# Token-major projections 512 columns at a time with four accumulators in the second layer, two first units side by side, and weights in half tiles

## The chip, the cores and the metric

The kernel runs on one core of one Trainium2 chip. The metric is the device time of one execution in microseconds (us); lower is better. A kernel's time is the median of several runs. The profile is of one further execution, and its times are the ones that a trace can explain line by line.

## What is computed

A trunk of two layers over 1024 tokens of width 1024, all in float32. Layer 0 projects the normed input and feeds a gated DeltaNet group and a sparse attention group (an indexer selects keys by score); layer 1 feeds a stick-breaking attention group and an HGRN2 gated recurrence. In each layer the two groups' outputs are concatenated and projected, and a SwiGLU FFN follows. Each mixer and each FFN is wrapped in two RMS norms, one ahead of it and one on its output before the residual is added:

```python
def rms_norm(x, g, eps=1e-6):
    xf = x.astype(jnp.float32)
    y = xf * lax.rsqrt(jnp.mean(xf * xf, axis=-1, keepdims=True) + eps)
    return (y * g.astype(jnp.float32)).astype(x.dtype)
...
    h = x
    for l in range(DEPTH):
        y = rms_norm(h, norm_g[l, 0])
        ...
        h = h + rms_norm(y, norm_g[l, 1])
        y = swiglu(rms_norm(h, norm_g[l, 2]), w_gate[l], w_up[l], w_down[l])
        h = h + rms_norm(y, norm_g[l, 3])
    return h
```

The even mixer's projection has 4176 columns, the odd one's 3584 (q, k, v of 512 each for the sticks; q, f, i and the output gate of 512 each for HGRN2). The FFN's inner width is 2816.

## The kernel before, in words

**Halves and tiles.** The 1024 tokens are worked on in two halves of 512. Activations lie feature-major: a half of h or y is 8 tiles of 128 features x 512 tokens. Weights come from HBM in "units" of 128 x 1024 floats, 422 in all; `wload` (L228) loads one raw unit (`wraw`) and splits it into a high part `whi` (ScalarE, L193) and a rest `wlo` (L197: VectorE for the first 512 columns, GpSimd for the second). Activations are split in the same way (`yhi`, `ylo`, or `act`). A product is then three passes on TensorE: high x high, low x high, high x low, added in one PSUM accumulator. `passes` (L240) issues them, at L251.

**Two kinds of projection.** `dense_fm` (L264) makes a feature-major result: one unit, one accumulator of 128 x 512, 24 matmuls of 512 columns. `dense_tm` (L270), called by `tm_store` (L541), makes a token-major one: 256 columns of the weights at a time, two accumulators each holding two token tiles, 48 matmuls of 256 columns to a unit. Four units make one token-major projection. In the second layer these are VC (values of the sticks, of both halves), ID (HGRN2's input) and GD (its gate); `tm_store` scales each result by the row form of the norm, passes it through a `stage` tile (two buffers) and stores it to HBM.

**PSUM.** There are 8 banks. `self.banks(acc=3, a=1, b=1, w=3)` in `run` (L1283) gives 3 to the accumulators, 1 to the recurrences' tag "a", 1 to tag "b", 3 to the attention's tag "w". Tiles of one tag are given out in the order in which the program asks for them: a tile waits until the one that had its bank before is read out.

**Norms.** A norm sums squares over the 8 feature tiles: ScalarE squares (L298), VectorE adds (L299, `ssq`). `inv_rms` (L302) adds over the partitions with one matmul by ones (L306), and ScalarE makes the inverse root by Ln and Exp (L308, L309); `inv_rms_rows` (L312) makes the same as a column for each token tile with four one-column matmuls (L317). Bank "b" serves them in `norms` (L346), `residual` (L376: scale L388, add h L389, store, then either make y's parts at once, L336, or square for the next norm) and `last_residual` (L504: L515, L516). The outputs of the output projection and the FFN are first gathered in `part` tiles by ScalarE (L429) or VectorE (L480, in the last FFN half L500).

**What sets the order.** The program is written half by half in `run`. A scheduler then lays out each engine's instructions by data, priorities (`with self.first()` gives a high one) and its own simulation; each engine runs its instructions in that order. So a matmul on bank "b" may be laid out far behind or ahead of matmuls on the accumulators, while two matmuls that start tiles of one tag keep the program's order. In the second layer the written order is: output projection of the first layer's second half, its residual, C projections (`proj_c`), sticks, FFN, its residual, second layer's output projection of half 0 (its first two quarters written ahead of that residual's second part), `proj_c(1)`, `proj_d(1)`, sticks and recurrence of half 1, FFN, output projection of half 1, and the last FFN, which goes by column halves (`down_halves`) with `last_residual` behind it.

## Time and profile before

| | |
|---|---|
| time, median of 3 runs (lowest to highest) | 2910.11 us (2907.5 to 2910.74) |
| the profiled execution's own time | 2903.69 us |
| its span on the core | 2901.9 us |
| mean granted TensorE clock | 0.992 |
| ScalarE busy | 1574.0 us (54%) |
| GpSimd busy | 1123.3 us (39%) |
| data moved by the hardware queue | 363.97 MB, 39.6% of its engines' span |

A row of the profile names the engine (PE is TensorE's matmuls, PEld its weight loads, DVE VectorE, ACT ScalarE, POOL GpSimd, SP the engine that issues the DMAs), the line, the tile written and the tiles read, the shape, and a count. A float32 matmul that is not split, such as a norm's by ones, stands as two records. In the timeline the first number is the start in us, the second the length; brackets give the idle time before a row and what ended it. In a view by windows each engine has its busy time and its count.

### The profile page before, as it was taken

What the parts mean: (1) busy time and instruction counts of PE and PEld (TensorE: products, weight loads), DVE (VectorE), ACT (ScalarE), POOL (GpSimd) and SP (SyncE); (2) the same over time, 40 slices, a digit from 0 to 9 for tenths busy, and PEclk for the clock granted to TensorE, in tenths of its full rate; (3) what the DMA queues carried; (4) which work ended last, traced back from release to release, by engine and by line L of the source; (5) the groups of instructions that cost most, each with busy time, mean ns of one, the idle gap of its engine ahead of it and who ended that gap; (6) DMA issues with size and microseconds to landing.
All of it is one profiled execution on the core that took longest, in us unless ns stands there. A gap on an engine that the chain in (4) does not pass through costs nothing. (4 is left out here: it accounts for less than half of the span.)

```text
span 2901.9 us, 41648 instructions
## 1 busy us (share of the span) xinstructions
PE 2818.6 (97%) x14850; PEld 2351.2 (81%) x14850; DVE 1694.5 (58%) x3037; ACT 1574.0 (54%) x2893; POOL 1123.3 (39%) x916
## 2 busy tenths in 40 slices
PE   8999999999999998999999999999999999999997
PEld 6888888878787886978788888889778778788886
DVE  7857973675656557378665235736666544732235
ACT  5545863666657585254664335536666544543333
POOL 3323332344435342255554332325555432333332
PEclk9999999999999999999999999999999999999999
DMA  5433446243333334446333334654323323543233
GB/s 196 136 121 109 144 151 209 91 146 114 103 117 107 104 121 137 139 147 202 111 109 95 100 97 125 231 156 128 98 87 107 98 89 115 167 149 98 95 95 109
DMA packets 200975, 366.63 MB, mean 126 GB/s; under 512 B 16544, under 2 KB 104640, under 8 KB 200768
## 3 DMA queue, kind: packets, MB, share of 16 engines
q1 hardware_dynamic: 200768, 363.97, 39.6%
q8 instruction: 117, 1.92, 0.3%
q14 instruction: 90, 0.74, 0.1%
HBM read 306.23 MB, written 57.67 MB: 125 GB/s over the span
## 5 line engine op out<-in xcount | busy, mean ns | idle before, releaser
L197 POOL TENSOR_TENSOR wlo<-wraw,whi 128x512 fp32r<-128x512 f32 x422 | 589.1, 1396 | 1240.3 <-PE acc L251 497.3
L193 ACT ACTIVATE whi<-wraw 128x512 fp32r<-128x512 f32 x844 | 521.6, 625 | 487.0 <-PE acc L251 431.2
L197 DVE TENSOR_TENSOR wlo<-wraw,whi 128x512 fp32r<-128x512 f32 x422 | 337.9, 801 | 470.7 <-PE acc L251 355.5
L251 PE MATMUL acc<-yhi,whi 128*128 128x512 f32 x2064 | 585.3, 400 | 11.8 <-ACT whi L193 8.0
L251 PE MATMUL acc<-ylo,whi 128*128 128x512 f32 x2064 | 581.9, 398 | 2.2 <-DVE ylo L336 2.2
L251 PE MATMUL acc<-yhi,wlo 128*128 128x512 f32 x2064 | 536.1, 396 | 0.0
L251 PE MATMUL acc<-act,whi 128*128 128x512 f32 (+1 forms) x1984 | 510.6, 393 | 21.3 <-DVE stage L452 5.7
L251 PEld LDWEIGHTS acc<-yhi,whi 128*128 128x128 f32 x2064 | 386.1, 189 | 99.5 <-ACT whi L193 8.0
L251 PEld LDWEIGHTS acc<-ylo,whi 128*128 128x128 f32 x2064 | 386.3, 189 | 88.3 <-issue 6.0
L251 PEld LDWEIGHTS acc<-yhi,wlo 128*128 128x128 f32 x2064 | 383.7, 188 | 84.1 <-issue 6.1
L251 PEld LDWEIGHTS acc<-act,whi 128*128 128x128 f32 x1984 | 363.1, 189 | 109.3 <-issue 11.5
L251 PE MATMUL acc<-act,wlo 128*128 128x512 f32 (+1 forms) x992 | 266.6, 386 | 1.4 <-POOL wlo L197 1.4
L251 PEld LDWEIGHTS acc<-act,wlo 128*128 128x128 f32 x992 | 182.0, 188 | 38.5 <-POOL wlo L197 1.8
L950 ACT ACTIVATE pen<-sc,tk 128x384 bf16<-128x384 f32 (+4 forms) x155 | 155.3, 1002 | 52.2 <-DVE tk L954 46.1
L480 DVE TENSOR_TENSOR part<-acc,part 128x512 f32<-128x512 f32 x152 | 103.8, 685 | 66.2 <-PE acc L251 66.0
L193 ACT ACTIVATE act<-stage 128x512 fp32r<-128x512 f32 x104 | 65.2, 629 | 136.9 <-DVE stage L459 117.0
L197 POOL TENSOR_TENSOR act<-stage,act 128x512 fp32r<-128x512 f32 x88 | 120.2, 1366 | 43.1 <-ACT act L193 41.0
L299 DVE TENSOR_TENSOR ssq<-ssq,sq 128x512 f32<-128x512 f32 (+1 forms) x119 | 98.7, 830 | 27.2 <-ACT sq L298 25.0
L951 DVE TENSOR_SCALAR tk<-tk 128x1 uint32<-128x1 f32 x186 | 39.3, 211 | 125.4 <-ACT pen L950 124.9
L452 DVE TENSOR_TENSOR stage<-acc,stage 128x512 f32<-128x512 f32 x66 | 45.5, 689 | 98.3 <-ACT stage L220 98.2
L251 PE MATMUL acc<-whi,yhi 128*128 128x256 f32 x640 | 100.1, 287 | 1.6 <-DVE stage L552 1.6
L251 PE MATMUL acc<-whi,ylo 128*128 128x256 f32 x640 | 101.3, 287 | 0.0
(461 smaller groups left out, 4038.1 us busy)
## 6 DMA issues: line engine op xcount, KB each, us to landing
wraw<-in_w_units_dram SPq DMA_DIRECT2D x422, 512.0 KB, 3.6
h<-part SPq DMA_DIRECT2D x40, 256.0 KB, 3.9
hld<-h SPq DMA_DIRECT2D x40, 256.0 KB, 4.6
qkvT<-stage SPq DMA_DIRECT2D x24, 256.0 KB, 2.5
kT<-kbT SPq DMA_DIRECT2D x24, 256.0 KB, 3.6
vv<-vb SPq DMA_DIRECT2D x24, 256.0 KB, 3.0
qkv<-qkvT SPq DMA_DIRECT2D x18, 256.0 KB, 3.6
part<-in_x_dram SPq DMA_DIRECT2D x16, 256.0 KB, 6.3
```

Of the source, the lines that this page charges most:

```text
L193: nc.scalar.activation(hi, src, AF.Copy)
L197: e.tensor_tensor(out=lo[:, c], in0=src[:, c], in1=hi[:, c].bitcast(F32), op=OP.subtract)
L251: mm(ps, l, r, start=first and g not in begun, stop=last and end[g] == i)
L299: nc.vector.tensor_tensor(out=acc, in0=acc, in1=sq, op=OP.add)
L452: nc.vector.tensor_tensor(out=s, in0=pg, in1=s, op=OP.mult)
L480: nc.vector.tensor_tensor(out=parts[d], in0=ps, in1=parts[d], op=OP.add)
L950: sc.activation(pen, s, AF.Sign, scale=sg, bias=nb, accum_out=n)
L951: v.tensor_scalar(rej.bitcast(U32), n, th, float(1 << b), op0=OP.is_lt, op1=OP.mult)
```

## The change

Layer 1 (from the point where the first layer's pools close) gets four accumulators and no bank "b". The norms that are made there use the accumulators' tag (`self.nb`); the first layer keeps bank "b". With four accumulators `tm_store` calls `dense_tm4`: all 512 columns at once, one accumulator for each token tile, 24 matmuls of 512 columns to a unit. The weights of that projection are read in other pieces from the same units. The raw weights come as two half tiles of 128 x 512 with a DMA each. `passes` takes its high pass in `steps` parts with the sums side by side, and its low pass one sum after the other. At the start of the kernel `dense_pair` runs two units (KI and the first QKV unit) side by side, in eight steps; the constants `cc` are loaded behind the first half's x.

```diff
@@ -156,7 +156,6 @@
         self.gg = self.t(cp, [P, G_COLS], "gg")
         with self.first():
             nc.sync.dma_start(self.gg, self.ins["p_cols"])
-            nc.sync.dma_start(self.cc, self.ins["c_main"])
         self.k = self.t(self.np_, [P, 8], "kk")
         nc.vector.memset(self.k[:, 0:1], -0.5)
         nc.vector.memset(self.k[:, 1:2], 1e-6)
@@ -225,27 +224,35 @@
         self.sigmoid(sig, dst)
         nc.vector.tensor_tensor(out=dst, in0=dst, in1=sig, op=OP.mult)
 
-    def wload(self, u):
+    def wload(self, u, tm=None):
+
         nc = self.nc
         with self.first():
-            raw = self.t(self.wp, [P, 1024], "wraw")
-            nc.sync.dma_start(raw, self.ins["w_units"][u])
             w = []
             for c, e in ((slice(0, 512), nc.vector), (slice(512, 1024), nc.gpsimd)):
-                w.append(self.split(raw[:, c], *(self.t(self.wp, [P, 512], n, F32R, bufs=4) for n in ("whi", "wlo")), (e,)))
+                raw = self.t(self.wp, [P, 512], "wraw", bufs=4)
+                if tm is None:
+                    nc.sync.dma_start(raw, self.ins["w_units"][u][:, c])
+                else:
+                    o = tm % 2 * 512 + c.start // 2
+                    src = self.ins["w_units"][u + tm // 2:u + tm // 2 + 3:2][:, :, o:o + 256]
+                    nc.sync.dma_start(raw.rearrange("p (c n) -> p c n", c=2), src.rearrange("c p n -> p c n"))
+                w.append(self.split(raw, *(self.t(self.wp, [P, 512], n, F32R, bufs=4) for n in ("whi", "wlo")), (e,)))
         self.pace()
 
         return lambda o, n=P: [t[:, o % 512:o % 512 + n] for t in w[o // 512]]
 
-    def passes(self, sums, w, first=True, last=True):
+    def passes(self, sums, w, first=True, last=True, steps=2):
 
 
 
         mm = self.nc.tensor.matmul
         order = [((0, 0), (0, 1)), ((1, 0),)] if w == 0 else [((0, 0), (1, 0)), ((0, 1),)]
-        n = len(sums[0][2]) // 2
-        seq = [(g, ps, l[a], r[b]) for pairs in order for part in (slice(0, n), slice(n, None))
-               for a, b in pairs for g, ps, terms in sums for l, r in terms[part]]
+        n = len(sums[0][2]) // steps
+        parts = [slice(i * n, (i + 1) * n) for i in range(steps)]
+        high, low = order
+        seq = [(g, ps, l[a], r[b]) for part in parts for a, b in high for g, ps, terms in sums for l, r in terms[part]]
+        seq += [(g, ps, l[a], r[b]) for a, b in low for g, ps, terms in sums for l, r in terms]
         begun, end = set(), {g: i for i, (g, *_) in enumerate(seq)}
         for i, (g, ps, l, r) in enumerate(seq):
             mm(ps, l, r, start=first and g not in begun, stop=last and end[g] == i)
@@ -266,6 +273,12 @@
         ps = self.acc()
         self.passes([(0, ps, [(w(k * P), y.t[k]) for k in range(KD)])], 0)
         return ps
+
+    def dense_pair(self, us, y):
+
+        ws, pss = [self.wload(u) for u in us], [self.acc() for _ in us]
+        self.passes([(i, ps, [(w(k * P), y.t[k]) for k in range(KD)]) for i, (w, ps) in enumerate(zip(ws, pss))], 0, steps=KD)
+        return pss
 
     def dense_tm(self, u0, y):
 
@@ -280,6 +293,15 @@
             for i in range(2):
                 yield 2 * i, c * n, ps[i]
 
+    def dense_tm4(self, u0, y):
+
+        ps = [self.acc() for _ in range(NT)]
+        for i in range(4):
+            w = self.wload(u0, i)
+            self.passes([(tt, ps[tt], [([t[:, tt * P:(tt + 1) * P] for t in y.t[2 * i + j]], w(j * 512, 512))
+                                       for j in range(2)]) for tt in range(NT)], 1, i == 0, i == 3)
+        return ps
+
     def rstd(self, pool, ss, n, width, tag):
         r = self.t(pool, [P, width], tag)
         self.nc.vector.tensor_scalar(r, ss, 1.0 / n, 1e-6, op0=OP.mult, op1=OP.add)
@@ -348,9 +370,9 @@
         acc = None
         for k in range(KD):
             acc = self.sumsq(acc, k, tiles[k])
-        y.r = self.inv_rms(acc, "rd", "b")
+        y.r = self.inv_rms(acc, "rd", self.nb)
         if rows:
-            y.rows = self.inv_rms_rows(acc, "b")
+            y.rows = self.inv_rms_rows(acc, self.nb)
 
     def part(self):
         if self.tail is not None:
@@ -368,6 +390,8 @@
                 else:
                     acc = self.sumsq(acc, k, x)
                 tiles.append(x)
+            if half == 0:
+                self.nc.sync.dma_start(self.cc, self.ins["c_main"])
             if half:
                 return self.to_y(0, 0, tiles, self.inv_rms(acc))
             self.norms(y, tiles, True)
@@ -377,7 +401,7 @@
 
         nc = self.nc
         with self.first():
-            r = self.inv_rms(acc, "rs", "b")
+            r = self.inv_rms(acc, "rs", self.nb)
             acc = None
             y = Y()
             for k in range(KD):
@@ -398,7 +422,7 @@
         if nxt is not None and not late:
             yield
             with self.first():
-                r = self.inv_rms(acc, "rs", "b")
+                r = self.inv_rms(acc, "rs", self.nb)
             yield
             with self.first():
                 box.append(self.to_y(*nxt, parts, r))
@@ -509,7 +533,7 @@
                 hs.append(self.t(self.tail, [P, HS], "tail"))
                 nc.sync.dma_start(hs[k], src[k * P:(k + 1) * P])
             for i, (c, acc) in enumerate(halves):
-                r = self.inv_rms(acc, ("rs", "rd")[i], "b")
+                r = self.inv_rms(acc, ("rs", "rd")[i], self.nb)
                 for k in range(KD):
                     p, h = parts[k][:, c], hs[k][:, c]
                     nc.vector.scalar_tensor_tensor(p, p, self.ng(1, 3, k), r, op0=OP.mult, op1=OP.mult)
@@ -541,6 +565,20 @@
     def tm_store(self, u0, y, dst, gain=None):
         nc = self.nc
         n = HS // 2
+        if self.shares["acc"] == NT:
+            for tt, ps in enumerate(self.dense_tm4(u0, y)):
+                with self.first():
+                    s = self.t(self.hp, [P, HS], "stage", bufs=2)
+                    if y.rows is None:
+                        nc.vector.tensor_copy(s, ps)
+                    else:
+                        nc.vector.tensor_scalar(s, ps, y.rows[:, tt:tt + 1], None, op0=OP.mult)
+                    if gain is not None:
+                        self.silu(s)
+                        s3 = s.rearrange("p (h d) -> p h d", h=NH)
+                        nc.gpsimd.tensor_tensor(out=s3, in0=s3, in1=gain[:, None, :].broadcast_to([P, NH, P]), op=OP.mult)
+                    nc.sync.dma_start(dst[tt * P:(tt + 1) * P], s)
+            return
         for tt, c0, ps in self.dense_tm(u0, y):
             with self.first():
                 s = self.t(self.hp, [P, HS], "stage", bufs=2)
@@ -570,7 +608,7 @@
             nc.vector.memset(self.hist, 0.0)
             self.ab = self.t(self.cp, [P, 8, 16], "ab")
             self.an = self.head_gain(self.cp, "a_norm")
-        ps = self.dense_fm(U_KI, y)
+        ps, first = self.dense_pair((U_KI, U_QKV), y) if half == 0 else (self.dense_fm(U_KI, y), None)
         with self.first():
             s = self.t(self.hp, [P, HS], "stage", bufs=2)
             if y.r is None:
@@ -584,7 +622,7 @@
             nc.vector.tensor_copy(self.ab[:, half * 4:half * 4 + 4, :],
                                   pt[:, 0:64].rearrange("p (t c) -> p t c", t=4))
         for ct in range(12):
-            ps = self.dense_fm(U_QKV + ct, y)
+            ps = first if half + ct == 0 else self.dense_fm(U_QKV + ct, y)
             with self.first():
                 xp = self.t(self.small, [P, HS + 3], "xp")
                 nc.vector.tensor_copy(xp[:, 0:3], self.hist[:, ct, :])
@@ -1281,6 +1319,7 @@
         every = lambda gen: deque(gen, maxlen=0)
         self.dn = self.head_gain(self.cp, "d_norm")
         self.banks(acc=3, a=1, b=1, w=3)
+        self.nb = "b"
         m0 = ExitStack()
         pool = m0.enter_context(tc.tile_pool(name="m0", bufs=1))
         self.small = m0.enter_context(tc.tile_pool(name="s0", bufs=1))
@@ -1314,6 +1353,8 @@
         self.proj_d(0, y[1])
         self.finish()
         m0.close()
+        self.banks(acc=4, a=1, w=3)
+        self.nb = "acc"
         m1 = ExitStack()
         pool = m1.enter_context(tc.tile_pool(name="m1", bufs=1))
         self.small = m1.enter_context(tc.tile_pool(name="s1", bufs=1))
```

What it moves on the engines is seen in the instructions' order. TensorE, between the first layer's last FFN half and the second layer's output projection of half 0 (`acc` tiles read from `act` and weights are that projection's, `b_17022` is the norm of the FFN's output, `b_17122` the norm of the new h, `b_17127` its row form). Before, around the first of these norms:

```order
L251 MATMUL acc_17184<-act_17162,whi_17221 128x512
L251 MATMUL acc_17184<-act_17168,whi_17221 128x512
L251 MATMUL acc_17183<-act_17173,whi_17225 128x512
L251 MATMUL acc_17184<-act_17173,whi_17225 128x512
L306 MATMUL b_17022<-ssq_16871,cc_76 128x512
L251 MATMUL acc_17262<-act_17137,whi_17266 128x512
L251 MATMUL acc_17262<-act_17143,whi_17266 128x512
```

The first norm stands between matmuls of the output projection. Another 122 rows on, before, the second:

```order
L251 MATMUL acc_17422<-act_17149,wlo_17431 128x512
L251 MATMUL acc_17422<-act_17155,wlo_17431 128x512
L306 MATMUL b_17122<-ssq_17099,cc_76 128x512
L251 MATMUL acc_17422<-act_17161,whi_17460 128x512
L251 MATMUL acc_17422<-act_17167,whi_17460 128x512
```

It too stands within the projection; the row form follows 23 rows later. In the changed kernel the same place on TensorE (`acc_17393` is the FFN's last accumulator, `acc_17410`, `acc_17510` and `acc_17515` the three norms, `acc_17571` and `acc_17572` the first of the output projection):

```order
L258 MATMUL acc_17393<-act_17055,wlo_17367 128x512
L258 MATMUL acc_17393<-act_17139,wlo_17373 128x512
L258 MATMUL acc_17393<-act_17223,wlo_17373 128x512
L328 MATMUL acc_17410<-ssq_17253,cc_76 128x512
L328 MATMUL acc_17510<-ssq_17487,cc_76 128x512
L339 MATMUL acc_17515<-cc_76,ssq_17487 128x1 x4
L258 MATMUL acc_17571<-act_17525,whi_17575 128x512
L258 MATMUL acc_17571<-act_17531,whi_17575 128x512
L258 MATMUL acc_17572<-act_17525,whi_17575 128x512
```

All three stand between the FFN's last matmul and the projection's first, with nothing between them. The other place is the norm ahead of the first layer's second FFN half. On TensorE before it stood within the C projections of half 0:

```order
L251 MATMUL acc_13546<-ylo_2384_11244,whi_13542 128x512
L251 MATMUL acc_13546<-ylo_2387_11253,whi_13542 128x512
L306 MATMUL b_13902<-ssq_13288,cc_76 128x512
L251 MATMUL acc_13546<-ylo_2390_11262,whi_13542 128x512
L251 MATMUL acc_13546<-ylo_2393_11271,whi_13542 128x512
```

In the changed kernel it stands on TensorE behind the last matmul of the token-major VC projection (`acc_14000`, `acc_14001`); eight matmuls of the recurrence ("a") follow, and then the FFN's first (`w_14210` belongs to a stick, `a_12827` to the recurrence):

```order
L258 MATMUL acc_14000<-wlo_14119,yhi_2532_11550 128x512
L258 MATMUL acc_14001<-wlo_14113,yhi_2529_11541 128x512
L258 MATMUL acc_14001<-wlo_14119,yhi_2532_11550 128x512
L1098 MATMUL w_14210<-qc_14203,kc_14205 128x128
L1263 MATMUL a_12827<-cc_76,kd_12730 128x128 x4
L328 MATMUL acc_14158<-ssq_13620,cc_76 128x512
L1270 MATMUL a_12834<-state_12673,qg_12725 128x128
L1271 MATMUL a_12834<-vi_12695,att_12733 128x128
```

It moved from the middle of the projections to their end. On VectorE, the four evictions of VC now stand directly ahead of the scalings of that norm (one weight split and one step of a stick lie between; `rc_11587` is the row form, `rs_14160` the norm):

```order
L575 TENSOR_SCALAR stage_14146<-acc_13998,rc_11587 128x512
L575 TENSOR_SCALAR stage_14149<-acc_13999,rc_11587 128x512
L196 TENSOR_TENSOR wlo_14683<-wraw_14680,whi_14682 128x512
L575 TENSOR_SCALAR stage_14152<-acc_14000,rc_11587 128x512
L1104 SCALAR_TENSOR_TENSOR ca_14217<-cz_14212 128x128
L575 TENSOR_SCALAR stage_14155<-acc_14001,rc_11587 128x512
L364 SCALAR_TENSOR_TENSOR part_13349<-part_13349,gg_77,rs_14160 128x512
L364 SCALAR_TENSOR_TENSOR part_13353<-part_13353,gg_77,rs_14160 128x512
```

## The prediction

> **What bounds the kernel now.** I read the page first, then the list of waits of TensorE, then windows and the timeline around the places that the change touches. The page's top says which engine sets the time:
>
> ```profile
> span 2901.9 us, 41648 instructions
> PE 2818.6 (97%) x14850; PEld 2351.2 (81%) x14850; DVE 1694.5 (58%) x3037; ACT 1574.0 (54%) x2893; POOL 1123.3 (39%) x916
> ```
>
> TensorE is busy for 2818.6 of 2901.9 us; everything else has slack on average. So the time is TensorE's own work plus 83 us in which it waits. A change can win only by taking matmul time away or by shortening these waits, and loses wherever it makes TensorE wait anew. The list of waits (total us, times, longest) shows how small and scattered they are:
>
> ```profile
> PE acc L251 <- ACT whi L193: 8.0, 1, 8.0
> PE a L744 <- DVE dec L740: 7.0, 1, 7.0
> PE b L306 <- DVE ssq L299: 5.8, 5, 2.9
> PE acc L251 <- DVE stage L452: 5.7, 2, 3.5
> PE acc L251 <- DVE part L500: 3.3, 2, 2.4
> ```
>
> The largest is the start (8.0 us). The norm matmuls of L306 wait only 5.8 us together: before hides the norms almost wholly. That is the fact on which this prediction turns.
>
> **The wider matmuls (gain).** Two windows full of one kind of work, after their header:
>
> ```profile
> core 0: us, PE busy (x) PEld busy (x) DVE busy (x) ACT busy (x) POOL busy (x), PEclk, DMA share, GB/s
> 1600.00:1650.00 50.00, 50.00 (x222) 41.40 (x221) 15.55 (x23) 18.24 (x30) 15.44 (x13) 1.00 0.30 95
> 1950.00:2000.00 50.00, 50.00 (x413) 49.44 (x412) 32.89 (x49) 27.42 (x48) 23.93 (x21) 1.00 0.47 140
> ```
>
> At 512 columns 222 matmuls take 50 us, 225 ns each. In the second window nearly all are 256 columns wide: 50/413 = 121 ns each, and the weight loads fill it (49.44 of 50 us), so two narrow matmuls cost more than one wide. A unit of 48 narrow ones takes 48 x 0.120 = 5.8 us, one of 24 wide ones 24 x 0.225 = 5.4 us. Four calls of four units change (VC of both halves, ID and GD of the second): 16 x 0.35 = about **-5 us**.
>
> **The norms in the accumulators (loss).** The four accumulators take the bank "b", and the second stage's norms now take their bank from "acc". In both kernels the accumulators start on TensorE in the order in which the program asks for them, so a norm's matmul can no longer be slipped into a later dense stream: it stands where the code asks. The worst place is between the first layer's last FFN and the second layer's output projection (rows in the section on the change): first norm, residual, second norm and its row form now follow one another with nothing between, where before 122 projection matmuls ran between the first two. What that chain takes is seen in before, where it was covered. TensorE's three norm matmuls, and VectorE around them:
>
> ```profile
> 1799.39 1.02 PE L306 MATMUL b<-ssq,cc 128*128 128x512 f32 x2
> 1829.02 1.12 PE L306 MATMUL b<-ssq,cc 128*128 128x512 f32 x2 [0.91 <-DVE ssq L299]
> 1835.24 0.95 PE L317 MATMUL b<-cc,ssq 128*128 128x1 f32 x8
> 1793.74 0.68 DVE L480 TENSOR_TENSOR part<-acc,part 128x512 f32<-128x512 f32 x1
> 1801.84 6.43 DVE L388 SCALAR_TENSOR_TENSOR part<-part,gg,rs 128x512 f32<-128x512 f32 x8 [1.99 <-ACT rs L309]
> 1808.19 1.89 DVE L389 TENSOR_TENSOR part<-part,hld 128x512 f32<-128x512 f32 x3
> 1810.60 1.48 DVE L336 SCALAR_TENSOR_TENSOR ylo<-part,gg,yhi 128x512 fp32r<-128x512 f32 x2
> 1810.00 0.68 DVE L197 TENSOR_TENSOR wlo<-wraw,whi 128x512 fp32r<-128x512 f32 x1
> 1825.15 0.68 DVE L197 TENSOR_TENSOR wlo<-wraw,whi 128x512 fp32r<-128x512 f32 x1
> 1828.28 1.28 DVE L299 TENSOR_TENSOR ssq<-ssq,sq 128x512 f32<-128x512 f32 x2
> ```
>
> (An "x2" of L306 is one matmul in two records.) The last eviction of the FFN starts at 1793.74 and the scaling at 1801.84; from there to the second norm matmul, 1829.02, are 27.2 us. Foreign work in that stretch is four weight splits (L197, first and last above) and an addition for the projection's own norm, 5 x 0.60 = 3.0 us; it cannot stand there any more, since it follows from projection matmuls that now come later. That leaves 24.2 us. Ahead of the scaling the shortest chain is eviction 0.68, addition 0.64, norm matmul 0.5, and the two ACT steps with their handovers, about 2.5: 4.3 us in place of 8.1. So the second norm can start 28.5 us after the last FFN matmul. TensorE does some 0.5 us of work in that gap, and the old wait of 0.91 us goes: 27.1 us. After such a gap TensorE runs slowly, as the page's existing gap of this sort shows:
>
> ```profile
> 1106.81 1.11 PE L744 MATMUL a<-cc,qkv 128*128 128x128 f32 x4 [6.95 <-DVE dec L740]
> 1102.00:1106.00 4.00, 0.00 (x0) 0.00 (x0) 4.00 (x6) 0.63 (x1) 2.65 (x3) 0.50 0.30 114
> 1106.00:1110.00 4.00, 3.19 (x9) 2.00 (x10) 2.60 (x9) 1.25 (x3) 0.14 (x1) 0.50 0.17 50
> ```
>
> After 6.95 us without a matmul the granted clock stays 0.50 for some 3.5 us, which costs 1.7. Together **+29 us**. Bounds: were VectorE to run its 8 scalings, 8 additions, 8 splits and 7 sums back to back (steps of 0.80, 0.60, 0.74 and 0.60: 6.4 + 4.8 + 5.9 + 4.2 = 21.3 us), the gap would be 4.3 + 21.3 - 1.4 + 1.7 = 26; keeping all the foreign work gives 8.1 + 27.2 - 1.4 + 1.7 = 36. I take 29, next to the measured chain.
>
> Four shorter waits of the same make. Three norms of an output projection or an FFN stand directly behind their last matmul (after the second layer's two output projections, and after its first FFN). The chain from an accumulator to the sum of squares:
>
> ```profile
> 1838.89 1.09 ACT L429 ACTIVATE part<-acc 128x512 f32<-128x512 f32 x2 [0.23 <-PE acc L251]
> 1839.86 1.15 ACT L298 ACTIVATE sq<-part 128x512 f32<-128x512 f32 x2
> 1840.52 1.55 DVE L299 TENSOR_TENSOR ssq<-ssq,sq 128x512 f32<-128x512 f32 x2 [1.34 <-ACT sq L298]
> ```
>
> 0.55 + 0.6 + 0.65 for the last tile, with handovers 2.2 us: 3 x 2.2 = **+6.6**; the fourth, behind the first layer's second output projection, has 8 small matmuls to cover it, **+1.2**. They are bounded by 0 and, with VectorE behind on other work, by 4 each.
>
> The second FFN half of the first layer: its norm (ready since long) now stands behind the VC projection, directly ahead of the FFN that needs it. After VC's last matmul VectorE makes four evictions, the third of which waits for the first of two stage buffers to be stored, then 8 scalings, and only then the low parts that the FFN's ninth matmul needs:
>
> ```profile
> vc<-stage SPq DMA_DIRECT2D x8, 256.0 KB, 3.5
> L342 DVE SCALAR_TENSOR_TENSOR part<-part,gg,rs x24: 735/740/1793, 254.5 to 1886.8; 128x512 f32<-128x512 f32 x24
> ```
>
> The first accumulator is done 1.4 us ahead of the last, is evicted 0.7 us later and stored some 3.5 us after that: the third and fourth evictions end about 4.2 us behind the last matmul; 8 scalings of 0.74 make 10.1, the first low part 11.4. TensorE has the norm (0.5), 8 recurrence matmuls (0.9) and 8 FFN matmuls (1.8) in between, so some 8 us idle, less what the sticks' matmuls fill: **+7.5 us**. Below, 3 (if the scalings come ahead of the held evictions); above, 11 (if nothing fills and the store takes 3 us more).
>
> **The start (gain).** TensorE's first matmul, the first QKV unit and the second:
>
> ```profile
> 8.04 0.80 PE L251 MATMUL acc<-yhi,whi 128*128 128x512 f32 x1 [8.04 <-ACT whi L193]
> 24.91 1.84 PE L251 MATMUL acc<-yhi,whi 128*128 128x512 f32 x4
> 33.34 1.09 PE L251 MATMUL acc<-yhi,whi 128*128 128x512 f32 x4
> ```
>
> Before, KI runs alone from 8.04 at the pace at which x arrives, then come its norm and transposes, then QKV 0, from 24.91 to 33.34: 8.4 us, partly at the lower clock and with small matmuls of the biases in between. Now both units run side by side from the first x tile, so QKV 0's 16 high matmuls fall into the waits for x. Its 8 low ones remain, at 0.30 us (between full and half rate) 2.4 us: 2.4 - 8.4 = **-6 us**. Bounds: -8.4 if all is hidden, -3 if its 24 matmuls are all paid (5.4 us); four half tiles of weights now stand ahead of six of the x tiles on SP, while the constants' load goes behind them.
>
> **The tail.** TensorE's last waits and VectorE's last work:
>
> ```profile
> 2883.49 1.19 PE L251 MATMUL acc<-act,whi 128*128 128x256 f32 x8 [2.40 <-DVE part L500]
> 2886.01 1.22 PE L251 MATMUL acc<-act,whi 128*128 128x256 f32 x8 [0.85 <-DVE part L500]
> 2890.60 0.70 PE L306 MATMUL b<-ssq,cc 128*128 128x256 f32 x2 [2.89 <-DVE ssq L299]
> 2878.75 4.26 DVE L515 SCALAR_TENSOR_TENSOR part<-part,gg,rs 128x256 f32<-128x256 f32 x8
> 2892.29 3.25 DVE L515 SCALAR_TENSOR_TENSOR part<-part,gg,rd 128x256 f32<-128x256 f32 x8 [1.75 <-ACT rd L309]
> 2895.46 2.76 DVE L516 TENSOR_TENSOR part<-part,tail 128x256 f32<-128x256 f32 x8
> ```
>
> Before, the first column half's norm comes early, and its 8 scalings hold VectorE just when evictions are due (the waits of 2.40 and 0.85). Its norm now stands 9 matmuls ahead of the end: these two waits go (-3.3), but half of that half's scalings and additions (6.0 us by the last two rows) falls behind the last eviction, of which the second norm's wait covers some: net **-1.8**, between -3.3 and +2.7.
>
> **Half tiles, pass order, four accumulators.** The weights come in 844 DMAs of 256 KB in place of 422 of 512 KB. SP's price for one, their landing, and the splits that follow them:
>
> ```profile
> 7.36 0.33 SPq L232 DMA_DIRECT2D wraw<-in_w_units_dram  x1
> wraw<-in_w_units_dram SPq DMA_DIRECT2D x422, 512.0 KB, 3.6
> L193 ACT ACTIVATE whi<-wraw 128x512 fp32r<-128x512 f32 x844 | 521.6, 625 | 487.0 <-PE acc L251 431.2 <-DMA wraw<-in_w_units_dram 37.0 <-issue 13.2
> ```
>
> SP's 422 further issues take 422 x 0.33 = 139 us over a span of 2900. The splits wait for TensorE 431 us and for the load 37 us, so loads run ahead; a unit of 5.4 us has a landing of 3.6 and a DMA share of 0.30 in the steady window. I price it at **0**, from -2 to +10, the cover being the depth of four half tiles: where a pair lands over 5.4 us after its buffers came free, the difference is paid in each unit. The Trainium skill ("DMA: Bandwidth & Descriptors", section "Bandwidth") speaks against the edit: it wants DMAs batched to at least 1 MiB, and a unit's two loads would, as an estimate from its table of sizes, take more of the queues than the one before; by that the sum would rise towards the +10 above. No run here has a 256 KB weight load yet. More accumulators remove small waits on evictions (5.7 us on L452 and the like), **-2**; the doubled use of two stage buffers by four evictions at once (ID to GD, GD to the FFN) gives about as much back, **+2**.
>
> **The sum**, against the profiled execution's own 2903.7 us (span 2901.9 and 1.8 around it): -5 + 29 + 6.6 + 1.2 + 7.5 - 6 - 1.8 + 0 - 2 + 2 = +31.5, so 2935. That execution lies 6.4 us below the median 2910.1, so the forecast is about **2941 us**, slower by 1.1%. The gains alone are some 13 us; the norm chain alone outweighs them twice.
>
> **The rivals.**
> 1. *The norms' waits are filled* (the other side). If TensorE passed the waiting norm and did the projection matmuls whose weights and activations are there, as the planner of before let it, the 29, 6.6, 1.2 and 7.5 us would vanish: 2903.7 - 13 = 2891, or 2897 as a median, faster. It decides at the point where less than about 13 us of the 44 remain. Against it: before's row at 1829.02, where TensorE waits 0.91 us for a sum of squares while the projection matmuls behind it, whose operands were split, do not pass. The Trainium skill ("TensorE: Matmul & The Clock Gate", section "Architectural detail: the array is 16× 32×32, not 1× 128×128") calls TensorE's queue a partial reorder window that pulls weight loads ahead; by a reading of it that lets matmuls pass as well, the time would be this rival's 2897. 5%.
> 2. *The chain is cheap*: VectorE runs dense (26), the FFN half's stall is 3, the others 1 each and the start gains 8: 26 + 3 + 4 - 8 - 5 - 3.3 - 2 = +15, median about 2925. For it: VectorE has nothing else in the gap; against it: the old chain's own waits for loads of h. 20%.
> 3. *More stalls*: the chain keeps its foreign work (36), the FFN half 11, the four short waits 4 each, and half tiles cost 5: 36 + 11 + 16 + 5 - 5 - 3 = +60, median about 2970. For it: the residual's loads of h go through three buffers only. 12%.
> 4. *The loads become the bound*: landing slower by over 1 us in every tight unit would add tens of us. The wait of 37 us on loads, off TensorE's path, speaks against it: 3%, 2980.
>
> **How the numbers follow.** The forecast, 2930 to 2955, holds 60%; rival 2 20%, rival 3 12%, rival 4 3%, rival 1 5%. The range of 8 in 10 goes from 2920 to 2962: it leaves out rival 1, rival 4, and the outer parts of 2 and 3. A measurement of this kernel tells 0.2% (5.8 us) from no change: faster 0.05, same (within 2904 to 2916) 0.04, slower 0.91.
>
> **What would show it.** In the changed profile: a wait of TensorE of 24 to 36 us on the sum of squares (the line of the norm matmul) at around 1800 us, with the clock at 0.50 behind it; three more of 2 to 3 us on that line; a wait of 3 to 11 us for the low parts of y near 1390 us; wide matmuls at 225 ns in the windows of the token-major units; QKV 1 starting near 26 us. The prediction is wrong if the chain's wait is under 12 us, or if TensorE's waits for weights, now 8 us at the start alone, grow into tens.

## The result, and the profile after

| | before | changed |
|---|---|---|
| median of 4 runs (lowest to highest) | 2908.81 us (2907.41 to 2910.74) | 2949.76 us (2945.59 to 2955.08) |
| profiled execution, span on the core | 2901.9 us | 2953.3 us |
| mean granted TensorE clock | 0.992 | 0.980 |

The changed kernel is slower: the ratio is 1.0141, with a 95% interval of 1.0123 to 1.0159, or 41 us. The forecast was 2941 with a range of 2920 to 2962. The profiled execution of the changed kernel is the slowest of its four, so its trace shows some 5 us more than the median.

The head of the changed kernel's page, to be set beside that of before:

```profile
span 2953.3 us, 41572 instructions
PE 2832.6 (96%) x14466; PEld 2344.8 (79%) x14466; DVE 1669.4 (57%) x3021; ACT 1581.4 (54%) x2893; POOL 1124.7 (38%) x916
PEclk9999999999999999999999997999999999999998
```

TensorE issues 384 records fewer and is nevertheless busy for 14 us longer (2832.6 against 2818.6), and it idles for 121 us instead of 83. The one 7 in its row of clocks, in slice 25 of 40, lies at 1772 to 1846 us. Both say the same: TensorE waits at new places and then runs slowly. The list of its waits (total us, times, longest) names the places:

```profile
PE acc L328 <- DVE ssq L321: 39.6, 7, 23.1
PE acc L258 <- DVE stage L590: 9.0, 2, 8.5
PE acc L258 <- ACT whi L192: 7.4, 3, 5.9
PE w L1115 <- POOL cal L1112: 5.9, 2, 4.7
```

The first row is the forecast's mechanism: the norm's matmul (L328, L306 of before) waits 39.6 us where it waited 5.8. The second row was not forecast. The longest wait of the third row is the start, 5.9 in place of 8.0. The fourth belongs to a stick and comes up again below.

TensorE's timeline at the long chain:

```profile
1804.65 1.07 PE L258 MATMUL acc<-act,wlo 128*128 128x512 f32 x4
1809.00 2.08 PE L328 MATMUL acc<-ssq,cc 128*128 128x512 f32 x2 [3.28 <-DVE ssq L321]
1834.14 2.07 PE L328 MATMUL acc<-ssq,cc 128*128 128x512 f32 x2 [23.07 <-DVE ssq L321]
1836.01 1.71 PE L339 MATMUL acc<-cc,ssq 128*128 128x1 f32 x8
```

The last FFN matmul ends at 1805.7 and the second norm's starts at 1834.1: 28.4 us, where 28.5 was reckoned. The last weights split ahead of the gap were ready by 1807.8 (GpSimd, L196) and the projection's last `act` by 1812.6 (VectorE, L196). So the projection matmuls behind the norms had their operands and did not pass. Three other norms wait 2.86, 3.21 and 2.44 us behind a projection or an FFN. And the switch of the banks:

```profile
1251.57 5.79 PE L258 MATMUL acc<-act,whi 128*128 128x512 f32 x16 [8.54 <-DVE stage L590]
```

The first projection matmul after the switch waits 8.54 us for the last eviction (L590) of the D projections in front of it.

### The profile page after: what moved, and what is told of

Same layout as the page of the kernel before. It is cut to its first block, busy times and chain, and to the rows that moved or that the text cites. A ratio compares the mean times of both kernels' runs of the same rounds, so it can differ in the third digit from the quotient of the medians.

```text
span 2953.3 us, 41572 instructions
## 1 busy us (share of the span) xinstructions
PE 2832.6 (96%) x14466; PEld 2344.8 (79%) x14466; DVE 1669.4 (57%) x3021; ACT 1581.4 (54%) x2893; POOL 1124.7 (38%) x916
## 5 line engine op out<-in xcount | busy, mean ns | idle before, releaser
L196 POOL TENSOR_TENSOR wlo<-wraw,whi 128x512 fp32r<-128x512 f32 x422 | 585.6, 1388 | 1334.5 <-PE acc L258 597.3
L196 DVE TENSOR_TENSOR wlo<-wraw,whi 128x512 fp32r<-128x512 f32 x422 | 333.7, 791 | 490.8 <-PE acc L258 366.3
L258 PEld LDWEIGHTS acc<-act,whi 128*128 128x128 f32 x1984 | 369.8, 192 | 93.6 <-ACT sq L219 8.7
L196 POOL TENSOR_TENSOR act<-stage,act 128x512 fp32r<-128x512 f32 x88 | 122.0, 1387 | 39.0 <-ACT act L192 35.5
L258 PE MATMUL acc<-whi,yhi 128*128 128x256 f32 (+1 forms) x512 | 98.7, 315 | 2.2 <-ACT whi L192 1.4
L258 PE MATMUL acc<-whi,ylo 128*128 128x256 f32 (+1 forms) x512 | 97.0, 312 | 0.0
```

What stands on the lines that cost most here:

```text
L196: e.tensor_tensor(out=lo[:, c], in0=src[:, c], in1=hi[:, c].bitcast(F32), op=OP.subtract)
L258: mm(ps, l, r, start=first and g not in begun, stop=last and end[g] == i)
```

## The experiments

Each median stands beside runs of the kernel before on the same chip. That kernel's median was 2907.27 us beside norms_in_w, switch_only, first_edits_only and norms_in_acc_only; 2910.53 beside other_banks, half_only, start_and_order and fourth_from_b; and 2909.62 beside chain_in_w, switch_early, half_and_fourth and norms_w_narrow. The theory was that the loss comes of the norms' place in the accumulators' order; the rivals, that wide evictions, half tiles or the bank switch bring it.

### The norms on another tag

```diff
         self.banks(acc=4, a=1, w=3)
-        self.nb = "acc"
+        self.nb = "w"
```

> The changed kernel with the second layer's norms on the attention's tag w in place of the accumulators' tag; all else as changed. Theory (the norms stand in the accumulators' order): the wait of 23 us on the sum of squares near 1834 us and most of the six shorter ones (16 us) go, with the slow clock behind them: 38 to 46 us less than the changed kernel, a median of 2904 to 2912. Rival (wide evictions, half tiles or the bank switch make the loss): less than 10 us gained, above 2940.

Measured: 2893.71 us (2891.93 to 2896.53), ratio to before 0.9945, 0.9924 to 0.9967. One word takes 56 us off the changed kernel and makes it faster than before. That is more than the 38 to 46 expected. TensorE's row in the head of this run's page tells why:

```profile
PE 2815.6 (97%) x14466; PEld 2336.6 (81%) x14466; DVE 1687.7 (58%) x3021; ACT 1582.0 (55%) x2893; POOL 1118.1 (39%) x916
```

Over a span of 2894.4 us TensorE idles for 78.8 us where the changed kernel idles for 120.7: 42 us less. It issues as many records (14466), but is busy for 17.0 us less (2815.6 against 2832.6): in the changed kernel the same number of matmuls runs more slowly. (Together 59 us; each of the two profiled executions is the slowest of its kernel.) The windows show where. The same five stretches, first in the changed kernel, then with the norms on w (us, then each engine's busy time with its count, the granted clock, the share of the DMA engines, GB/s):

```profile
1880.00:1900.00 20.00, 17.14 (x67) 13.16 (x66) 12.69 (x18) 9.03 (x15) 5.00 (x2) 0.91 0.17 52
2490.00:2510.00 20.00, 16.79 (x60) 12.64 (x59) 13.51 (x20) 10.57 (x18) 4.12 (x2) 0.83 0.33 104
2570.00:2590.00 20.00, 17.56 (x69) 13.88 (x69) 10.87 (x18) 6.33 (x10) 6.06 (x3) 0.91 0.28 92
1386.00:1406.00 20.00, 11.89 (x50) 8.77 (x50) 14.21 (x25) 9.21 (x18) 7.68 (x5) 0.83 0.23 70
1800.00:1850.00 50.00, 23.66 (x82) 17.37 (x81) 30.67 (x46) 21.20 (x37) 4.41 (x3) 0.66 0.40 131
```

```profile
1880.00:1900.00 20.00, 20.00 (x89) 16.18 (x88) 11.66 (x17) 7.30 (x14) 5.36 (x5) 1.00 0.54 179
2490.00:2510.00 20.00, 20.00 (x90) 16.57 (x89) 18.50 (x26) 12.33 (x22) 8.63 (x5) 1.00 0.63 201
2570.00:2590.00 20.00, 20.00 (x90) 16.57 (x89) 3.05 (x5) 9.29 (x15) 4.24 (x4) 1.00 0.38 111
1386.00:1406.00 20.00, 20.00 (x106) 16.99 (x105) 9.44 (x17) 10.99 (x23) 6.86 (x8) 1.00 0.46 145
1800.00:1850.00 50.00, 50.00 (x222) 40.73 (x221) 40.94 (x51) 33.32 (x59) 14.21 (x9) 1.00 0.58 185
```

The reader should look at the counts of TensorE, the first number with an x. In the last stretch the changed kernel does 140 records fewer, at 225 ns each 31.5 us of work not done. In the first three it does 22, 30 and 21 fewer: 5.0, 6.8 and 4.7 us, though the waits in them are only 2.86, 3.21 and 2.44. The rest is mostly the slow clock behind each wait (0.91, 0.83 and 0.91 over these 20 us). The stretches don't hold the same work in both kernels, but in the first three and the last nearly all of it is 128x512 matmuls, so the counts can be compared.

### The long chain alone

```diff
         every(self.ffn(0, y[0], f))
         r = self.after_ffn(0, 1, f, y, True)
+        self.nb = "w"
         next(r)
+        self.nb = "acc"
```

> The changed kernel with only the three norms between the first layer's last FFN half and the second layer's output projection on tag w; the other norms of the second layer stay on the accumulators' tag. Theory: the long chain is 30 to 36 us of the 56 between the changed kernel and norms_in_w (its waits of 26.4 us and the slow clock after them), so 2914 to 2920; the remaining 20 us are the short waits and the slow clock that each brings. Rival (the chain is nearly all of it): below 2905. Rival (the short waits are the larger part): above 2925.

Measured: 2919.98 us (2914.15 to 2922.14). That is 29.8 us below the changed kernel, at the lower edge of the 30 to 36 expected, and 26.3 above norms_in_w. So the long chain is a little over half of the norms' price. In its trace the wait on L328 is 26.4 us less; the short waits are still there (L328 waits 13.2 us in 5 pieces, the longest 4.4 at the tail), and so is the stall ahead of the FFN half.

### The bank switch

```diff
         m0.close()
+        self.banks(acc=3, a=1, b=1, w=3)
         m1 = ExitStack()
```

> The kernel before, with nothing but the banks given out anew (same shares) where the first layer's pools close. Theory (the new banks wait for the old ones' last evictions, held by two stage buffers): a wait of 5 to 9 us of TensorE at about 1245 us, and 5 to 9 us more than before. Rival (that wait comes of half tiles or pass order): no new wait there, within 2 us of before.

Measured: 2919.99 us (2918.17 to 2926.52), ratio 1.0039, 1.0027 to 1.0052: 8 to 15 us lost by giving the same banks out anew (12.7 by the medians), more than the 5 to 9 expected. The wait is the one of the changed kernel, here on the old lines; in before the row L552 has 1.6 us:

```profile
PE acc L251 <- DVE stage L552: 10.3, 2, 9.1
```

So the switch, and nothing else of the change, makes this wait. Two runs asked what it hangs on. First, other places for the tags in the new pool (this on top of norms_in_w):

```diff
         self.nb = "w"
+        self.mx("w"), self.mx("a")
```

> As norms_in_w, and one tile of w and one of a asked for (and left unused) directly behind the bank switch, so that these tags are given the lower banks and the accumulators others than before. Theory (the wait of 8.5 us behind the switch comes of the accumulators' place: the first new one lies on a bank whose last eviction is late): the wait at about 1250 us is under 2 us, and the median 8 to 12 us below norms_in_w (2893.7), so 2882 to 2886. Rival (the new banks as a whole wait for the last eviction in the old ones): the wait stays at 8 us or so, and the time within 2 us of norms_in_w.

Measured: 2894.38 us, ratio 0.9946 (0.9931 to 0.9961), the same as norms_in_w, and the wait stays at 8.5:

```profile
PE acc L258 <- DVE stage L590: 9.0, 2, 8.5
```

The rival's numbers came. Which bank each tag was given isn't seen in a trace, so that the place does not matter is likely but not shown. Second, the switch at another place (on top of norms_in_w; the D projections of half 0 are wide too):

```diff
+        self.banks(acc=4, a=1, w=3)
+        self.nb = "w"
         self.proj_d(0, y[1])
         self.finish()
         m0.close()
-        self.banks(acc=4, a=1, w=3)
-        self.nb = "w"
```

> norms_in_w with the bank switch moved ahead of the second layer's first D projections, behind the first layer's FFN, where evictions don't go through the two stage buffers; the D projections of half 0 are then wide too (8 more units, some 2.6 us). Theory (the 8.5 us are the wait for evictions held by stage stores): no wait over 4 us of TensorE at the switch, median 2880 to 2886. Rival (a switch costs such a wait wherever it stands, as all banks must be empty): 2890 to 2896.

Measured: 2909.37 us (2904.67 to 2913.05), ratio 0.9999: 16 us worse than norms_in_w, worse than either theory. The 8.5 us for the stage evictions are gone from its list, and TensorE waits inside the recurrences instead:

```profile
PE a L1251 <- POOL x L1235: 9.8, 3, 4.7
PE a L817 <- DVE tt L812: 6.2, 4, 3.0
PE a L880 <- DVE sq L873: 4.6, 1, 4.6
```

L817 and L880 are waits in the first layer's DeltaNet recurrence; L1251 is the second layer's HGRN2 recurrence, at 1353 and 1358 us, and why it waits longer isn't found here. Ahead of the early switch the DeltaNet recurrence is still running, and the D projections, which fill its waits in norms_in_w, need the new banks. TensorE's first matmul in them comes only at 1174.57 us:

```profile
1174.57 2.07 PE L258 MATMUL acc<-yhi,whi 128*128 128x512 f32 x4 [0.69 <-ACT sq L881]
```

What it waits for is the copy of the recurrence's last result out of bank "a" (L881). In both places the first new accumulator starts right behind the last reading of an old bank. This speaks for a switch as a barrier: the new accumulators wait until what stood in the old pool is done, wherever the switch stands. The prediction had no term for it.

### The first edits, together and apart

Without the new banks, so with narrow projections and norms on b:

```diff
-        self.banks(acc=4, a=1, w=3)
-        self.nb = "acc"
```

> The changed kernel without the new banks: three accumulators and bank b throughout, 256 columns in the token-major projections, norms on b; half tiles, pass order, the pair at the start and the later constants stay. Theory (these edits are worth the start's gain and otherwise nothing): 2 to 6 us less than before, QKV 1 starts 6 us earlier. Rival A (half tiles cost): 3 us or more slower than before. Rival B (start's gain is lost again where the first recurrence waits for other engines): within 1.5 us of before.

Measured: 2891.88 us (2886.38 to 2892.74), ratio 0.9933 (0.9906 to 0.9959): 15 us gained, more than any side expected. The half tiles alone, on the kernel before:

```diff
-            raw = self.t(self.wp, [P, 1024], "wraw")
-            nc.sync.dma_start(raw, self.ins["w_units"][u])
...
+                raw = self.t(self.wp, [P, 512], "wraw", bufs=4)
+                nc.sync.dma_start(raw, self.ins["w_units"][u][:, c])
```

> The kernel before with the raw weights in half tiles, a DMA each, and nothing else. Theory (the half tiles bring most of the 15 us that first_edits_only gained, since a half can be split while the other is on its way): 7 to 13 us less than before. Rival (they cost or bring nothing, the gain is the start's and the pass order's): within 3 us of before.

Measured: 2885.15 us (2882.79 to 2890.68), ratio 0.9916 (0.9901 to 0.9931): 25 us, about twice the most that was expected. The head of its page, and some of TensorE's waits in it:

```profile
span 2885.5 us, 42435 instructions
PE 2818.4 (98%) x14850; PEld 2353.0 (82%) x14850; DVE 1687.4 (58%) x3037; ACT 1578.0 (55%) x2893; POOL 1124.2 (39%) x916
```

```profile
PE acc L251 <- ACT whi L193: 8.1, 1, 8.1
PE a L734 <- ACT y L724: 5.7, 2, 3.6
PE acc L251 <- POOL act L197: 1.5, 4, 0.4
PE a L744 <- DVE dec L740: 0.5, 1, 0.5
```

TensorE's busy time is that of before to 0.2 us, and it idles for 67.1 us in place of 83.3. So the two traces show 16 of the 25 us; the profiled execution of before was itself 6 us faster than its median. The gain is waits that went: L744 from 7.0 to 0.5, GpSimd's `act` from 4.8 to 1.5, and the FFN's `stage` on L452 (5.7 before) is no longer in the list. Others grew: L734, in the same recurrence as L744, from 2.1 to 5.7. Waits for weights are hardly among those that went: `whi` at the start is 8.0 before and 8.1 here, and only one of 1.4 us on `wlo` is gone. How half tiles take the others away isn't shown. The rest of the change, on whole raw tiles:

```diff
             nc.sync.dma_start(self.gg, self.ins["p_cols"])
-            nc.sync.dma_start(self.cc, self.ins["c_main"])
...
+        ps, first = self.dense_pair((U_KI, U_QKV), y) if half == 0 else (self.dense_fm(U_KI, y), None)
```

> The kernel before with the pair of units at the start, the constants loaded later and the new pass order, but whole raw tiles and three accumulators. Theory: only the start's gain, 3 to 6 us less than before, the first QKV pair done some 4 us earlier. Rival: 10 us or more less than before, the half tiles being of no use. If the two parts add up, this and half_only together give first_edits_only's 15 us.

Measured: 2893.70 us (2892.39 to 2894.64), ratio 0.9942 (0.9927 to 0.9957): 17 us. The rival's size, then, but not in the rival's place of the half tiles: 25 and 17 apart, 15 together. The parts don't add up. Each alone takes idle time from TensorE (83.3 us before, 67.1 and 73.7 in these two traces), and each lays the program out anew; what their common order loses again isn't found here.

### All of the loss without the other edits

```diff
+        self.banks(acc=4, a=1, w=3)
+        self.nb = "acc"
...
-        y.r = self.inv_rms(acc, "rd", "b")
+        y.r = self.inv_rms(acc, "rd", self.nb)
```

> The kernel before with four accumulators and the norms in their tag from where the first layer's pools close (so with the bank switch), but narrow token-major projections, whole raw tiles and the old start. Theory: the whole loss is here, 40 to 55 us more than before, with a wait of 20 us or more on the sum of squares near 1830 us. Rival (the loss needs the wide projections or the half tiles): under 20 us more.

Measured: 2953.45 us (2950.43 to 2956.07), ratio 1.0149 (1.0117 to 1.0180): the whole loss, without the wide projections and the half tiles.

```profile
PE acc L306 <- DVE ssq L299: 41.3, 6, 23.4
```

The norm waits as in the changed kernel. With the switch's 12.7 us (switch_only on the same chip) taken off, the norms cost 33 us here and 56 in the changed kernel. Against switch_only TensorE idles for 33 us more here and is busy for 1 us more; in the changed kernel, against norms_in_w, it was 42 and 17. So most of the difference is that records run more slowly in the changed kernel, and the last section comes back to it.

### Versions that keep the gains

No switch, norms on w, and the fourth accumulator from bank b:

```diff
-        ps = [self.acc() for _ in range(NT)]
+        ps = [self.acc() for _ in range(NT - 1)] + [self.mx("b")]
...
+        self.nb, self.four = "w", True
```

> A version meant to keep the gains and drop the losses: the banks of before throughout (no switch); in the second layer the norms go to w and the wide token-major projections take bank b as their fourth accumulator; half tiles, pair and pass order as changed. Theory: first_edits_only (2891.9) less the 5 us of the wider matmuls, 2884 to 2890, and no wait above 4 us at 1250 us. Rival (the wide projections' evictions through two stage buffers eat their gain): 2891 or more.

Measured: 2883.16 us (2877.51 to 2886.37), ratio 0.9910 (0.9893 to 0.9926): 27 us faster than before, 67 faster than the changed kernel, a microsecond beyond what was expected. The same with narrow projections:

```diff
-        self.nb, self.four = "w", True
+        self.nb, self.four = "w", False
```

> fourth_from_b with the token-major projections 256 columns at a time as before, so it differs in the wide projections alone. Theory (16 units of 0.35 us): 4 to 6 us above fourth_from_b (2883.2), 2887 to 2889. Rival (the wide projections gain nothing after their evictions): within 2 us of it.

Measured: 2890.65 us (2889.18 to 2892.93), ratio 0.9938 (0.9921 to 0.9954), so 7.5 us for the wide projections, somewhat above the 4 to 6 expected. TensorE's busy time is 6.4 us less with them (2808.8 against 2815.2), so most of this is matmul time, as reckoned. And with the start and the pass order of before:

```diff
-        ps, first = self.dense_pair((U_KI, U_QKV), y) if half == 0 else (self.dense_fm(U_KI, y), None)
+        ps = self.dense_fm(U_KI, y)
```

> fourth_from_b with the start and the pass order of before (no pair, constants loaded early), so half tiles, norms on w and wide projections with bank b as the fourth accumulator. Theory (the pair and the pass order cost some us where the half tiles are there, as half_only at 2885.2 against first_edits_only at 2891.9 says): 2874 to 2879. Rival (that difference is only the order that the planner happened on): 2881 or more.

Measured: 2890.07 us (2887.79 to 2890.35), ratio 0.9931 (0.9916 to 0.9946). The theory failed: without the pair the version is 7 us slower, not faster, though half_only had been 7 us faster than first_edits_only (their intervals overlap). So the 7 us between such versions are not the price of the pair. Nor do gains carry over: this version is half_only with wide projections and norms on w, and it isn't faster than half_only. half_only (0.9916) and fourth_from_b (0.9910) can't be told apart by their intervals; they are the best two.

## Why the prediction was right, and where its sizes were off

**The mechanism and the sign were right.** The norms' matmuls stand in the accumulators' order and TensorE waits for them. The rival that TensorE passes a waiting norm is out: it waited 23.07 us while projection matmuls with finished operands stood behind. The waits in sum came out as reckoned: 42.4 us for all places together, and TensorE idles for 42 us more than in norms_in_w. **The slow clock behind them was mis-sized**: the sum had 1.7 us for it, and the busy time of the same 14466 records differs by 17.0. So the norms cost 56 us where 44 were forecast. The long chain was put at 29 us and measured as 29.8 (the changed kernel less chain_in_w). Its parts were less exact: the gap is 28.4 us, as reckoned, but the slow clock behind it cost more than the 1.7 us given to it. Three windows of the changed kernel, the granted clock third from the end:

```profile
1834.00:1838.00 4.00, 3.86 (x11) 2.83 (x12) 0.09 (x1) 1.57 (x3) 0.00 (x0) 0.50 0.06 24
1838.00:1842.00 4.00, 4.00 (x11) 3.03 (x11) 0.00 (x0) 0.85 (x3) 0.00 (x0) 0.50 0.00 0
1842.00:1846.00 4.00, 4.00 (x17) 3.28 (x16) 0.64 (x1) 0.63 (x2) 0.15 (x1) 0.91 0.00 0
```

Half of 8 us and a tenth of 4 are 4.4 us.

**The short waits were mis-sized**, by the clock again. The sum had 6.6 us for three norms: the waits measure 8.5, and by the records not done in their three stretches (73 at 225 ns) the loss is some 16. The step that failed is the one that priced a wait of 2 us at its length alone. The fourth norm, put at 1.2, waited 0.3.

**The stall ahead of the FFN half** was put at 7.5 and came as three waits (TensorE's timeline, changed kernel):

```profile
1389.22 2.72 PE L258 MATMUL acc<-yhi,whi 128*128 128x512 f32 x8 [1.25 <-ACT yhi L354]
1394.06 0.33 PE L1114 MATMUL w<-cah,lt 128*128 128x128 f32 x1 [2.12 <-ACT cah L1111]
1399.13 0.48 PE L1115 MATMUL w<-cal,lt 128*128 128x128 f32 x1 [4.75 <-POOL cal L1112]
```

Together 8.1 us, but not by the steps reckoned. The prediction had the low parts of y come last and let the sticks' matmuls fill the gap; here two of the three waits are a stick's (L1114, L1115). The other engines around them:

```profile
1387.77 5.38 DVE L364 SCALAR_TENSOR_TENSOR part<-part,gg,rs 128x512 f32<-128x512 f32 x8
1393.86 4.89 DVE L356 TENSOR_TENSOR ylo<-part,yhi 128x512 fp32r<-128x512 f32 x8
1394.09 4.99 POOL L1112 TENSOR_TENSOR cal<-ca,cah 128x128 fp32r<-128x128 f32 x1 [7.46 <-ACT cah L1111]
```

The stick's step on VectorE stands behind the eight scalings, and then GpSimd's `cal` takes 4.99 us, against a median of 1.27 over its 48 executions of all sizes; it runs while VectorE makes the low parts, but why it is slow isn't shown. The first low part was there at some 1394.5 us, so without the stick TensorE would have waited 2.6 us there in place of 6.9 (an estimate from these rows). That the sum of the three came close to 7.5 is luck. That VectorE's queue, which serves both, makes the delay is read from the order and wasn't tried.

**A term was missing**: the bank switch, which the prediction took as free. Alone it costs 12.7 us by the medians (1.0039, 8 to 15 us).

**A term was too small the other way**: half tiles at 0. Alone they gain 25 us. The prediction argued from loads that run ahead, and that holds: only 1.4 us of TensorE's waits for weights went. What it didn't see is that other waits of TensorE would change with the edit, and the runs leave open how. The Trainium skill ("DMA: Bandwidth & Descriptors", section "Bandwidth") wants large DMAs. Here DMAs of half the size landed in 2.7 us in place of 3.6, the hardware queue's share of its engines stayed (39.8% in half_only, 39.6% before), and the kernel became faster.

```profile
wraw<-in_w_units_dram SPq DMA_DIRECT2D x844, 256.0 KB, 2.7
```

**The start**: the second QKV unit begins earlier, as forecast, but on a slow clock (0.85 from 24 to 28 us, 0.72 from 28 to 32):

```profile
25.74 1.19 PE L258 MATMUL acc<-yhi,whi 128*128 128x512 f32 x4
26.77 1.85 PE L258 MATMUL acc<-ylo,whi 128*128 128x512 f32 x4
```

25.74 in place of 33.34 is 7.6 us, more than the 6 reckoned, but eight of its matmuls run at some 0.4 us each until 30 us, so part of it is given back at once: the third unit starts 6.1 us earlier (33.97, before 40.10). **The tail** waits 4.44 us once, where before waited 2.40, 0.85 and 2.89: 1.7 us less. But from the last norm's matmul (2940.81) to the end it is 12.5 us in place of 11.3, so the gain is 0.5 us, within the bounds but less than the 1.8 forecast. **The wide matmuls** gained 7.5 us by the two versions, 5 forecast.

So 2941 came close to 2950 with errors that partly cancel, which is luck: the switch (+12.7) was missing and the norms cost 12 us more than reckoned, mostly by the clock, while the first edits gained 9 us more than the 6 reckoned (first_edits_only, 15 us) and the wide projections 2.5 more. That leaves +13 where the forecast was 10 us short (31 against 41); the parts are from different kernels and need not add up exactly.

## What to carry to other kernels

Before a small operation is moved onto a shared tag of buffers, look where it then stands in that tag's order: a matmul that waits for a chain on other engines belongs on a tag on which nothing dense has to follow it. Giving all banks out anew acted as a barrier at both places tried, so it is better avoided, here by borrowing a bank. And a wait of TensorE of 2 to 3 us is to be priced between its length and about twice that: the clock may fall behind it.

## What was not expected of the hardware

Short waits lowered the clock, but not always. Three windows of the changed kernel around 3.21 us without a matmul (the granted clock is third from the end):

```profile
2492.00:2496.00 4.00, 0.79 (x2) 0.50 (x2) 2.68 (x3) 1.57 (x3) 1.32 (x1) 0.83 0.45 131
2496.00:2500.00 4.00, 4.00 (x9) 2.61 (x8) 1.22 (x2) 1.32 (x2) 0.00 (x0) 0.50 0.00 2
2500.00:2504.00 4.00, 4.00 (x16) 3.18 (x16) 4.00 (x7) 1.26 (x2) 0.00 (x0) 0.81 0.02 4
```

In the second row TensorE is busy all the time and does 9 matmuls instead of 18. But the same wait need not have this price. A norm waits 2.44 us in the changed kernel (until 2572.47) and in chain_in_w (until 2533.20); these are the windows 1.5 and 0.8 us behind the two waits' ends:

```profile
2574.00:2578.00 4.00, 4.00 (x13) 3.12 (x13) 2.69 (x5) 1.88 (x3) 0.00 (x0) 0.68 0.00 0
2534.00:2538.00 4.00, 4.00 (x18) 3.16 (x17) 2.25 (x4) 1.95 (x3) 0.00 (x0) 1.00 0.10 36
```

In chain_in_w the clock stayed at 1.00 there, and 18 matmuls were done in place of 13. In norms_in_acc_only a norm's wait of 2.80 us (until 2493.41) left the clock at 1.00 too, while a wait of 1.76 us in the same run (until 942.22) was followed by a clock of 0.72 from 944 to 948 us. In norms_in_w a wait of 3.70 us (until 160.38) left it at 1.00. The Trainium skill ("TensorE: Matmul & The Clock Gate", section "What's actually happening") has the low clock come after an idle window of about 3.4 us; as a limit on the length of a single wait this doesn't hold here, in either direction. What decides isn't shown. So a part of the price of the short waits, and of the difference between 33 and 56 us for the norms, doesn't follow from how long the waits are.

It was also not expected that two edits which gain 25 and 17 us alone gain 15 together. That the order which the scheduler happens on is worth so much is a reading; no run separates it from other causes.
